# A hybrid encoder layer on one core: the first row blocks multiplied for two column chunks in turn, and the conversions of the start reordered

## The chip, the cores and the metric

One core of a Trainium2 chip runs the whole layer in one launch. Five engines work side by side: TensorE (PE) multiplies, VectorE (DVE) and ScalarE (ACT) do elementwise work, GpSimd (POOL) sets a few constants, SyncE (SP) issues nearly all transfers from the chip's memory. The metric is the device time of an execution in microseconds. A measurement of this kernel can tell apart differences of about 0.2%, some 2.3 us.

## The reference, cut to what matters

The layer takes 256 tokens of 2048 channels in 32-bit floats. Only its first product is touched by the change:

```
hn = rms_norm(h, g_mix_pre)          # h: 256 x 2048
u = hn @ w_in                        # w_in: 2048 x 5120
q, k, v, xr, yg = split(u)           # 1024 columns each
attn = neighborhood_attention(q, k, v, rpb)
rec = rglru_bidirectional(xr, ...) * gelu(yg)
mixed = concat(rms_norm(attn), rms_norm(rec)) @ w_out
...                                  # SwiGLU FFN, gated embedding, sandwich norms
```

## The kernel before, in words

**Products.** Each 32-bit factor is held as two parts, a high one rounded to the matmul's format (`wh` for weights, `hT_hi` for activations) and the rest (`wl`, `hT_lo`). A product is three matmuls: high by high, high by `wl`, `hT_lo` by `wh`. PE does them for 128 tokens and 512 columns at a time, accumulating over the 2048 channels in 16 blocks of 128.

**Weight tiles.** `w_in` is cut into ten *chunks* of 512 columns. A chunk is worked through in eight weight tiles, each with a pair of channel blocks (two blocks of 128 rows by 512 columns, 512 KB). A block takes six matmuls (three products for each of two groups of 128 tokens), a tile twelve. Chunk 0 (part of `xr`) goes first, then chunk 1 (part of `v`), and so on. The name `acc` is the accumulators of a chunk, two banks of PSUM.

**Streams of a weight tile.** `load_stream` issues its transfer on SP into one of four buffers `wr`; `hi_stream` casts it on ACT to `wh`; `lo_stream` subtracts on DVE and gives `wl`. There are six buffers for `wh` and `wl`. `pieces(i)` says whether tile `i` is handled whole or in two halves (a half is one channel block). Before, only tile 0 is halved.

**x.** The activations come transposed, as `xs`: pair `k` of channel blocks ahead of weight tile `k`. `make_hT` scales each block on ACT (L311, `hT_hi`) and takes the rest on DVE (L313, `hT_lo`). The tokens once more, untransposed (`xn`), come ahead of tiles 8 to 11; `norm_x` sums their squares and gives `rstd_x`, by which the chunks' results are scaled when they leave `acc`. `decay` works out small constants (`la`, `c8`) for the recurrence. `warm_up` runs seven matmuls on zeros before any data is there.

**After a chunk.** Chunk 0 is scaled on ACT into `ev`, transposed on DVE, sent through memory (`via`) and back, and copied into `xp`; eight DVE steps of a convolution make `xc`, whose two parts `xch` and `xcl` go into the gate matmuls `pg`. Chunk 1 is scaled into `vh` on ACT (L1136) and `vl` on DVE (L1140).

**What sets the order.** Matmuls of the tiles are written out in order. All other work is in small tasks, and while the program is built, a planner (`Plan`) plays through a model of time with costs per operation: each time it takes the task that can start earliest, shifted by the task's `late` (negative is more urgent), and writes its next instruction. Each engine then works strictly in that written order. A task added with a ready time is not considered earlier. `plan.clk["dma"]` is the time from which the model's transfers run, at 340 KB per us with 2 us to landing.

## Time and profile before

| what | us |
|---|---|
| median of 3 runs | 1155.36 |
| lowest, highest | 1154.85, 1156.58 |
| the profiled execution | 1154.11 |
| its span, first to last instruction | 1152.3 |
| PE busy | 1137.1 |
| DVE busy | 973.5 |
| ACT busy | 701.1 |

The span is what the trace shows; the execution's own time is 1.8 us more. Matmuls are pipelined: one of 512 columns is shown with a duration of 0.39 us, while the next starts 0.23 us after it, so the pace is read from the starts. "Idle before" is the time for which an engine stood still ahead of an instruction, with what released it. SPq is the queue on which SP issues transfers. Weight tiles are counted from 0, matmuls of the accumulators from 1.

### The profile page before, as it was taken

How to read it: one execution, taken by the hardware profiler on the slowest of the kernel's cores; microseconds unless marked ns; L12 is line 12 of the kernel's file. 1: busy time of each engine (PE TensorE's matmuls, PEld its weight loads, DVE VectorE, ACT ScalarE, POOL GpSimd, SP SyncE). 2: the span in 40 equal slices, each digit the busy share in tenths (PEclk: the TensorE clock that was granted, in tenths of full speed). 3: DMA queues.
4: the chain of work that ended last, by engine and by line, in shares of the span. 5: the costliest groups of instructions: out<-in, count | busy, mean ns of one | idle time of the engine just before them, and what ended most of it. 6: DMA issues, size and time to landing. Idle time of an engine off the chain costs nothing.

```text
span 1152.3 us, 14571 instructions
## 1 busy us (share of the span) xinstructions
PE 1137.1 (99%) x5138; PEld 942.0 (82%) x5138; DVE 973.5 (84%) x1266; ACT 701.1 (61%) x939; POOL 1.6 (0%) x13
## 2 busy tenths in 40 slices
PE   8999999999999999999999999999999999999996
PEld 6888888887888888888888888888888888888885
DVE  6668788789558898999977889999987999888996
ACT  7776888866548645474455555556444556466863
POOL 0000000000000000000000000000000000000000
PEclk9999999999999999999999999999999999999999
DMA  9876766576974877577775675668675757875661
GB/s 342 294 227 194 261 206 199 152 233 192 346 224 162 279 231 260 190 250 238 235 225 173 201 241 184 210 229 267 204 241 178 218 188 224 303 278 209 185 199 73
DMA packets 83305, 257.68 MB, mean 224 GB/s; under 512 B 8992, under 2 KB 24736, under 8 KB 81824
## 3 DMA queue, kind: packets, MB, share of 16 engines
q1 hardware_dynamic: 83088, 256.67, 68.8%
q8 instruction: 40, 0.66, 0.2%
q14 instruction: 33, 0.27, 0.1%
q10 hardware_dynamic: 144, 0.08, 0.0%
HBM read 242.04 MB, written 14.68 MB: 223 GB/s over the span
## 4 chain that ended last, share of the span: by engine, by line
PE 91%; DVE 3%; DMA 2%; ACT 2%; issue 1%; SPq 1%; DVEq 0%; ACTq 0%
PE c L558 15%; PE c L556 15%; PE c L557 15%; PE acc L557 9%; PE acc L558 9%; PE acc L556 9%; PE p L565 3%; PE p L567 3%; PE p L566 3%; PE c L565 2%; PE c L567 2%; PE c L566 2%; DVE wl L518 1%; DMA ev<-via 1%; ACT wh L508 1%
## 5 line engine op out<-in xcount | busy, mean ns | idle before, releaser
L518 DVE TENSOR_TENSOR wl<-wr,wh 128x1024 fp32r<-128x1024 f32 (+1 forms) x315 | 364.7, 1178 | 58.0 <-ACT wh L508 57.0
L508 ACT CAST wh<-wr 128x1024 fp32r<-128x1024 f32 (+1 forms) x315 | 314.1, 1018 | 141.7 <-PE c L558 50.5
L556 PE MATMUL c<-wh,hT_mix_hi 128*128 128x512 f32 x412 | 160.7, 390 | 0.0
L558 PE MATMUL c<-wh,hT_mix_lo 128*128 128x512 f32 x412 | 160.4, 389 | 0.0
L557 PE MATMUL c<-wl,hT_mix_hi 128*128 128x512 f32 x412 | 160.3, 389 | 0.0
L508 ACT CAST wh<-lent_t 128x1024 fp32r<-128x1024 f32 x69 | 72.3, 1053 | 130.3 <-DVE lent_t L542 96.4
L556 PE MATMUL acc<-wh,hT_hi 128*128 128x512 f32 x320 | 126.4, 395 | 1.8 <-ACT wh L508 1.8
L557 PE MATMUL acc<-wl,hT_hi 128*128 128x512 f32 x320 | 125.5, 392 | 1.5 <-DVE wl L518 1.5
L558 PE MATMUL acc<-wh,hT_lo 128*128 128x512 f32 x320 | 125.4, 392 | 0.0
L518 DVE TENSOR_TENSOR wl<-lent_t,wh 128x1024 fp32r<-128x1024 f32 x69 | 83.1, 1220 | 13.3 <-ACT wh L508 12.8
L558 PEld LDWEIGHTS c<-wh,hT_mix_lo 128*128 128x128 f32 x412 | 77.3, 188 | 16.3 <-DVE hT_mix_lo L313 0.2
L557 PEld LDWEIGHTS c<-wl,hT_mix_hi 128*128 128x128 f32 x412 | 77.4, 188 | 15.9
L556 PEld LDWEIGHTS c<-wh,hT_mix_hi 128*128 128x128 f32 x412 | 77.3, 188 | 15.8
L557 PEld LDWEIGHTS acc<-wl,hT_hi 128*128 128x128 f32 x320 | 60.4, 189 | 14.7 <-DVE wl L518 2.9
L556 PEld LDWEIGHTS acc<-wh,hT_hi 128*128 128x128 f32 x320 | 60.5, 189 | 14.4 <-ACT wh L508 2.4
L558 PEld LDWEIGHTS acc<-wh,hT_lo 128*128 128x128 f32 x320 | 60.4, 189 | 12.7
L508 ACT CAST wh<-lent_r 128x1024 fp32r<-128x1024 f32 (+1 forms) x57 | 55.7, 989 | 24.7 <-PE c L558 21.4
L518 DVE TENSOR_TENSOR wl<-lent_r,wh 128x1024 fp32r<-128x1024 f32 (+1 forms) x57 | 64.8, 1142 | 5.0 <-ACT wh L508 4.9
L556 PE MATMUL c<-wh,mid1h 128*128 128x512 f32 x84 | 32.7, 389 | 0.0
L557 PE MATMUL c<-wl,mid1h 128*128 128x512 f32 x84 | 32.7, 389 | 0.0
L558 PE MATMUL c<-wh,mid1l 128*128 128x512 f32 x84 | 32.7, 389 | 0.0
L565 PE MATMUL p<-wh,sums_f 128*128 128x512 f32 x80 | 31.1, 389 | 0.0
(501 smaller groups left out, 2331.4 us busy)
## 6 DMA issues: line engine op xcount, KB each, us to landing
wr<-in_w_in SPq DMA_DIRECT2D x79, 512.0 KB, 4.6
wr<-in_w_ffn_down SPq DMA_DIRECT2D x70, 512.0 KB, 4.8
wr<-in_w_ffn_gate SPq DMA_DIRECT2D x64, 512.0 KB, 4.5
wr<-in_w_ffn_up SPq DMA_DIRECT2D x64, 512.0 KB, 4.4
wr<-in_w_out SPq DMA_DIRECT2D x32, 512.0 KB, 5.0
lent_r<-in_w_ffn_up SPq DMA_DIRECT2D x24, 512.0 KB, 3.9
lent_r<-in_w_ffn_gate SPq DMA_DIRECT2D x24, 512.0 KB, 4.5
wr<-in_w_ple_gate SPq DMA_DIRECT2D x24, 512.0 KB, 4.5
```

Of the source, the lines that this page charges most:

```text
L508: nc.scalar.copy(his[i][:, j, :], raws[i][:, j, :])
L518: nc.vector.tensor_tensor(out=los[i][:, j, :], in0=raws[i][:, j, :], in1=f32(his[i][:, j, :]), op=ALU.subtract,)
L556: nc.tensor.matmul(accs[t], hi[t], wh[:, j, :], start=st, stop=False)
L557: nc.tensor.matmul(accs[t], hi[t], wl[:, j, :], start=False, stop=False)
L558: nc.tensor.matmul(accs[t], lo[t], wh[:, j, :], start=False, stop=sp)
L565: nc.tensor.matmul(o, lh, wh, start=start, stop=False)
L566: nc.tensor.matmul(o, lh, wl, start=False, stop=False)
L567: nc.tensor.matmul(o, ll, wh, start=False, stop=stop)
```

## The change

It does five things, all at the start of the program.

1. Tiles 0 and 1 are now the first pair of channel blocks for chunk 0 and for chunk 1; then come the other seven pairs for chunk 0, then those for chunk 1. Both chunks' accumulators are open from the start.
2. Tiles 0, 1 and 2 are loaded and converted in halves.
3. The x pairs 1 to 7 are loaded ahead of tiles 2 to 8 (before: 1 to 7), the `xn` ahead of tiles 9 to 12.
4. `make_hT` is less urgent (-1.0, before -1.4), `decay` is ready only at 20, and the planner's model has transfers start at 0.7 and books 440 KB more ahead of tile 0's second half (nothing is transferred for it).
5. One more matmul on zeros stands behind the first six matmuls.

```diff
+TURNS = 1
+HALVED = 3
+DECAY = 20.0
+HT_LATE = -1.0
+XN_FROM = 9
+FIRST_KB = 440
+FILL = {(0, 0): 1}
...
-        return [slice(0, 1), slice(1, 2)] if i == 0 else [slice(0, 2)]
+        return [slice(0, 1), slice(1, 2)] if i < HALVED else [slice(0, 2)]
...
             for j in pieces(i) if i not in singles else [slice(0, 2)]:
+                if not i and j.start:
+                    yield dma(FIRST_KB)
...
                 free_w(i)
+            for _ in range(FILL.get((i, j), 0)):
+                dummy()
             plan.run()
...
-        for j in pieces(k):
-            extra_loads.setdefault((k, j.start), []).append(load_xs(k, j))
+        i = 2 * k if k < TURNS else k + TURNS
+        for j in [slice(0, 1), slice(1, 2)] if not i else [slice(0, 2)]:
+            extra_loads.setdefault((i, j.start), []).append(load_xs(k, j))
     for i in range(2 * NT):
-        extra_loads.setdefault((8 + i, 0), []).append(load_xn(i))
+        extra_loads.setdefault((XN_FROM + i, 0), []).append(load_xn(i))
...
+        if n == 1:
+            for k in KS[:TURNS]:
+                for ch, c0 in firsts:
+                    seg(ch, "w_in", c0, hT, [k], first=k == KS[0], last=False)
+            for ch, c0 in firsts:
+                seg(ch, "w_in", c0, hT, KS[TURNS:], first=not TURNS)
+        elif n:
+            seg(chunk, "w_in", n0, hT, KS, after=start_biases if n == 3 else None)
...
+    plan.clk["dma"] = 0.7
...
-    plan.add(make_hT(0), late=-2 * LATE)
-    plan.add(make_hT(1), late=-2 * LATE)
+    plan.add(make_hT(0), late=HT_LATE)
+    plan.add(make_hT(1), late=HT_LATE)
     plan.add(norm_x(), late=NORM_X)
-    plan.add(decay())
+    plan.add(decay(), DECAY)
```

Below, names carry the program's buffer numbers, which differ between the two builds, and line numbers of the changed kernel are 7 to 15 higher. SP at the start, before (`xs0` is the half of the x blocks with pairs 0 to 3; a row of 128x512 is half a weight tile or a whole x pair):

```order
L665 DMA xs0_80<-in_xT 128x256
L483 DMA wr_115<-in_w_in 128x512
L665 DMA xs0_80<-in_xT 128x256
L483 DMA wr_115<-in_w_in 128x512
L665 DMA xs0_80<-in_xT 128x512
L483 DMA wr_125<-in_w_in 128x1024
L665 DMA xs0_80<-in_xT 128x512
L483 DMA wr_140<-in_w_in 128x1024
```

and after:

```order
L676 DMA xs0_80<-in_xT 128x256
L492 DMA wr_114<-in_w_in 128x512
L676 DMA xs0_80<-in_xT 128x256
L492 DMA wr_114<-in_w_in 128x512
L492 DMA wr_131<-in_w_in 128x512 x2
L676 DMA xs0_80<-in_xT 128x512
L492 DMA wr_138<-in_w_in 128x512 x2
L676 DMA xs0_80<-in_xT 128x512
L492 DMA wr_156<-in_w_in 128x1024
```

Two halves of the next weight tile moved ahead of the second x pair. ACT at the start, before (L721 is the first step of `decay`):

```order
L721 ACT_TABLE_LOAD
L721 ACTIVATE la0_105<-vec_69 128x16
L311 ACTIVATE hT0_hi_78<-xs0_80,vec_69 128x256
L508 CAST wh_122<-wr_115 128x512
L311 ACTIVATE hT0_hi_78<-xs0_80,vec_69 128x256 x2
L508 CAST wh_122<-wr_115 128x512
L311 ACTIVATE hT0_hi_78<-xs0_80,vec_69 128x256
L508 CAST wh_144<-wr_125 128x1024
```

and after:

```order
L318 ACT_TABLE_LOAD
L318 ACTIVATE hT0_hi_78<-xs0_80,vec_69 128x256
L517 CAST wh_119<-wr_114 128x512
L318 ACTIVATE hT0_hi_78<-xs0_80,vec_69 128x256
L517 CAST wh_119<-wr_114 128x512
L517 CAST wh_147<-wr_131 128x512 x2
L318 ACTIVATE hT0_hi_78<-xs0_80,vec_69 128x256
L517 CAST wh_167<-wr_138 128x512
L318 ACTIVATE hT0_hi_78<-xs0_80,vec_69 128x256
L517 CAST wh_167<-wr_138 128x512
L318 ACTIVATE hT0_hi_78<-xs0_80,vec_69 128x256 x2
L517 CAST wh_194<-wr_156 128x1024
```

The second half tile's cast now stands behind one x block of its own pair, where it stood behind the first block of the next pair; `la` has left. DVE follows in the same order with `hT_lo` and `wl`. ACT at the end of chunk 1, before (L723 is decay's second step, L843 the copies into `xp`):

```order
L723 ACT_TABLE_LOAD
L723 ACTIVATE la0_105<-la0_105 128x16
L508 CAST wh_494<-wr_465 128x1024
L508 CAST wh_509<-wr_477 128x1024
L508 CAST wh_549<-wr_518 128x1024
L843 COPY xp_335<-ev_424 128x8x4x8 x2
L508 CAST wh_565<-wr_532 128x1024
L843 COPY xp_335<-ev_424 128x8x4x8
L1136 ACTIVATE vh_351<-acc0_367,rstd_x_84 128x512
L843 COPY xp_335<-ev_424 128x8x4x8
L1136 ACTIVATE vh_351<-acc1_368,rstd_x_84 128x512
L508 CAST wh_595<-wr_543 128x1024
```

and after:

```order
L735 ACT_TABLE_LOAD
L735 ACTIVATE la0_105<-la0_105 128x16
L517 CAST wh_527<-wr_489 128x1024
L517 CAST wh_543<-wr_508 128x1024
L1151 ACTIVATE vh_373<-acc0_158,rstd_x_84 128x512
L1151 ACTIVATE vh_373<-acc1_159,rstd_x_84 128x512
L858 COPY xp_357<-ev_452 128x8x4x8 x4
L517 CAST wh_614<-wr_541 128x1024
L517 CAST wh_627<-wr_565 128x1024
L517 CAST wh_633<-wr_581 128x1024
```

Both `vh` moved ahead of all four copies and of the casts of tiles 20 to 22. On PE the sequence of kinds of matmuls is the same as before but for the one on zeros; only the tiles' order in the first two chunks differs.

More of the change, by code (lines that the diff above doesn't have):

```diff
@@ L755, in decay, with dummy @@
         done(ev_c8)
+    some, to = xn[0][:, 0:P], bank("warm")[:, 0, 0:P]
+    def dummy():
+        nc.tensor.matmul(to, some, some, start=True, stop=True)
     def warm_up():
-        some = xn[0][:, 0:P]
         nc.vector.memset(some, 0.0)
-        to = bank("warm")[:, 0, 0:P]
         for _ in range(WARM):
-            nc.tensor.matmul(to, some, some, start=True, stop=True)
+            dummy()
     t1 = {}
@@ L1206, in start_biases @@
         plan.add(load_biases(), plan.clk["pe"])
+    firsts = []
     for n, (n0, post) in enumerate((
@@ L1213, in layer @@
         late = SOON if n >= SOON_FROM else 0.0
-        seg(Chunk(post, (open_p1, second_tiles)[n] if n < 2 else None, late), "w_in", n0, hT, KS,
-            after=start_biases if n == 3 else None)
+        chunk = Chunk(post, (open_p1, second_tiles)[n] if n < 2 else None, late)
+        if n < 2:
+            firsts.append((chunk, n0))
+        if n == 1:
[6 more added lines that the diff above has]
+            seg(chunk, "w_in", n0, hT, KS, after=start_biases if n == 3 else None)
+    last_in = len(segs) - 1
     t2 = {}
@@ L1917, in layer @@
             run_seg(s)
-            if n == 9:
+            if n == last_in:
                 ev_in.t = plan.clk["pe"]
```

## The prediction

> **What bounds the kernel now.** I read the engine shares first, then the waits of PE, then the chain of work, and last the first 16 us instruction by instruction. Whole page, one later window, and the waits of PE (us in total, times, longest):

> ```profile
> PE 1137.1 (99%) x5138; PEld 942.0 (82%) x5138; DVE 973.5 (84%) x1266; ACT 701.1 (61%) x939; POOL 1.6 (0%) x13
> ...
> 400.00:600.00 200.00, 200.00 (x884) 165.62 (x883) 182.86 (x214) 107.78 (x119) 0.00 (x0) 1.00 0.71 230
> ...
> PE acc L556 <- ACT wh L508: 1.8, 2, 1.1
> PE acc L557 <- DVE wl L518: 1.5, 3, 1.0
> ...
> PE pb_rec L968 <- DVE ssr L983: 0.7, 1, 0.7
> ```

> The middle of the kernel is matmuls end to end: 884 in 200 us, 0.226 us each. All of PE's waits on weight halves (1.8 and 1.5 us) are on `acc`, and the timeline puts them ahead of 12.5 us. What is left is far later and small, such as the 0.7 at `pb_rec`. So the change, which touches only the start, can win what the start loses and no more. The chain of work shows how that loss is made (start, us, what):

> ```profile
> 2.59 4.50 DMA xs<-in_xT
> ...
> 7.11 0.51 ACT hT_hi L311
> 7.62 0.51 ACT wh L508
> 8.12 0.41 ACT hT_hi L311
> 8.54 0.93 ACT wh L508
> ...
> 9.91 0.89 DVE hT_lo L313 x2
> 10.80 1.15 DVE wl L518
> ...
> 11.99 0.79 PE acc L557
> ```

> Until 7.1 us the chain waits for the second x block; then it goes through the conversions on ACT and DVE to 12 us. The same stretch in the timeline (start, duration, engine, idle before and its releaser):

> ```profile
> 1.05 3.21 PE L762 MATMUL warm<-xn 128*128 128x128 f32 x14 [1.05 <-DVE xn L759]
> ...
> 3.28 0.22 ACT L721 ACTIVATE la<-vec 128x16 f32<-128x16 f32 x1 [0.83 <-DMA vec<-in_vecs]
> 3.40 0.49 ACT L311 ACTIVATE hT_hi<-xs,vec 128x256 fp32r<-128x256 f32 x1
> ...
> 4.20 0.62 ACT L508 CAST wh<-wr 128x512 fp32r<-128x512 f32 x1 [0.31 <-DMA wr<-in_w_in]
> ...
> 4.85 0.69 DVE L518 TENSOR_TENSOR wl<-wr,wh 128x512 fp32r<-128x512 f32 x1 [0.44 <-ACT wh L508]
> ...
> 4.87 0.50 PE L556 MATMUL acc<-wh,hT_hi 128*128 128x512 f32 x1 [0.62 <-ACT wh L508]
> ...
> 5.60 0.50 PE L557 MATMUL acc<-wl,hT_hi 128*128 128x512 f32 x1 [0.23 <-DVE wl L518]
> ...
> 5.76 0.51 ACT L311 ACTIVATE hT_hi<-xs,vec 128x256 fp32r<-128x256 f32 x1 [0.94 <-DMA xs<-in_xT]
> ...
> 6.30 0.48 DVE L313 SCALAR_TENSOR_TENSOR hT_lo<-xs,vec,hT_hi 128x256 fp32r<-128x256 f32 x1 [0.75 <-ACT hT_hi L311]
> ...
> 6.63 0.40 PE L558 MATMUL acc<-wh,hT_lo 128*128 128x512 f32 x1
> ...
> 7.11 0.51 ACT L311 ACTIVATE hT_hi<-xs,vec 128x256 fp32r<-128x256 f32 x1 [0.84 <-DMA xs<-in_xT]
> 7.52 0.60 ACT L508 CAST wh<-wr 128x512 fp32r<-128x512 f32 x1
> ...
> 8.97 0.68 DVE L518 TENSOR_TENSOR wl<-wr,wh 128x512 fp32r<-128x512 f32 x1
> ...
> 9.71 0.50 PE L557 MATMUL acc<-wl,hT_hi 128*128 128x512 f32 x1 [1.03 <-DVE wl L518]
> ...
> 14.27 0.40 PE L556 MATMUL acc<-wh,hT_hi 128*128 128x512 f32 x1
> ```

> The first half tile is multiplied from 4.87 to 6.86. The seventh matmul could go when the second half is converted; but its cast stands on ACT behind the second x block (7.11), and on DVE its low half comes 8.97 to 9.65, behind three x blocks. So the eighth matmul starts at 9.71 and not some 2 us before. And then PE runs at half clock. PE busy, PEld, DVE, ACT, POOL, granted clock, DMA share and GB/s:

> ```profile
> 3.97:7.39 3.42, 2.22 (x9) 1.14 (x7) 1.62 (x3) 1.41 (x3) 0.00 (x0) 1.00 0.91 319
> 7.39:10.80 3.41, 1.59 (x6) 1.11 (x7) 2.46 (x6) 3.29 (x7) 0.00 (x0) 1.00 1.03 404
> 10.80:14.21 3.41, 3.15 (x8) 2.03 (x7) 3.41 (x6) 2.73 (x5) 0.00 (x0) 0.50 1.03 363
> 14.21:17.60 3.39, 3.39 (x16) 2.75 (x15) 3.00 (x5) 2.81 (x5) 0.00 (x0) 1.00 0.98 369
> ```

> The stretch in which PE was busy 1.59 of 3.41 us is followed by one of the same length at clock 0.50. From 14.27, the 19th matmul, nothing waits until far later. In this execution the start thus costs 14.27 - 18 x 0.227 = 10.18 us ahead of a stream that never stops.

> **The change, part by part.**

> *Order of loads.* The first four transfers stay. Fifth and sixth are now the halves of chunk 1's first weight tile, where the second x block (256 KB) and a whole tile stood. The fifth was 256 KB before and is so now, so it lands at 7.08 as the x block did. From then on I take 404 GB/s (row 7.39:10.80): 256 KB in 0.65 us. Landings: tile 1 at 7.08 and 7.73, x pair 1 at 8.38, tile 2 at 9.03 and 9.68, x pair 2 at 10.33. By the 363 GB/s of the next row, tile 3 (512 KB, 1.44 us) lands at 11.77. The two more issues on SP cost nothing as long as an issue is shorter than a landing (0.65); by the nearest row, four `ev` issues in 2.18 us further below, one takes 0.55, and were the two not hidden, it is 1.1 us.

> [...]

> *ACT and DVE at the start.* The small `la` activation leaves the front: 3.40 becomes 3.28, hidden, since the cast at 4.20 waits for its landing. The second half's cast moves ahead of the second x pair. It landed by about 6.45 (5.76 plus 0.65), so cast 6.48 to 7.08, low half 7.11 to 7.80: 1.85 us earlier than 9.65. The other ends, by the rows' durations (half cast 0.60, x block 0.50, half low 0.68, x low 0.48): tile 1's low halves at 8.4 and 9.1, x block 2 low 9.5, tile 2's at 10.3 and 11.3, x block 3 low 10.7, tile 3 (whole: cast about 1.0 from 11.8, low 1.2) at 14.1. Two halves in place of a whole cost ACT 1.2 for 1.0 and DVE 1.37 for 1.2, twice: all of it beside PE's work, which has 24 matmuls (5.4 us) on the first x pair instead of 12.

> *PE.* Matmuls 1 to 6 as before. The seventh could go at 7.13, the eighth, on the low half, at 7.85. The extra warm-up matmul is two instructions, each at most the 3.21 / 14 = 0.23 us of the first ones: 0.46 us from 6.86 to 7.32. Then the seventh goes 0.2 later and still ends ahead of 7.85, so the cost is nothing; without that wait it would be up to 0.46. Then tile 0 ends at 8.98; tile 1 needs 8.4 and 9.1 at 8.98 and 10.34; tile 2 needs 10.3 and 11.3 at 11.70 and 13.06; tile 3 needs 14.1 at 14.42. No wait, the last by 0.3 us. The 19th matmul starts at 7.85 + 11 x 0.227 = 10.34.

> **Sum:** 14.27 - 10.34 = 3.93 us. About 1.7 of it is the stretch at half clock (3.41 / 2), which goes because PE is busy from 7.85 on; the rest are the two longest waits (1.1 and 1.0 in the list) and a small one, less the 0.5 that PE still waits ahead of the eighth. The most that could be won: no wait after 5.60 puts the eighth matmul at 6.96, a gain of 4.8.

> *Decay later, norm later, chunks 0 and 1 nearer together.* The decay chain, ready at 20, stays off the path. Chunk 1 now ends at 7.85 + 185 x 0.227 = 49.8 instead of 53.7, and what hangs on it is the next thing that could be late:

> ```profile
> 42.03 2.18 SPq L349 DMA_DIRECT2D ev<-via  x4
> ...
> ev<-via SPq DMA_DIRECT2D x4, 128.0 KB, 6.1
> ...
> 51.70 1.22 ACT L843 COPY xp<-ev 128x256 f32<-128x256 f32 x2
> ...
> 54.31 0.67 ACT L1136 ACTIVATE vh<-acc,rstd_x 128x512 fp32r<-128x512 f32 x1
> ...
> 55.63 0.42 DVE L880 TENSOR_SCALAR xc<-xp,vec 128x256 f32<-128x256 f32 x1 [2.57 <-ACT xp L843]
> ...
> 57.49 0.75 DVE L1140 SCALAR_TENSOR_TENSOR vl<-acc,rstd_x,vh 128x512 fp32r<-128x512 f32 x1
> ...
> 64.65 0.69 DVE L307 TENSOR_TENSOR xcl<-xc,xch 128x512 fp32r<-128x512 f32 x1
> ...
> 67.34 0.28 PE L362 MATMUL pg<-xch,gh 128*128 128x256 f32 x1
> ```

> The gate matmuls (`pg`) stand after 252 matmuls, as before: needed at 7.85 + 245 x 0.227 = 63.4, not 67.3. ACT now does both `vh` (from 49.9), then the four `xp` copies, then three casts: copies end at 49.9 + 6 x 0.6 = 53.5. From the first `xc` to the end of `xcl` it was 65.34 - 55.63 = 9.7 us; one weight half (1.15) and two `vl` (1.3) leave that stretch, four small decay steps of at most 0.48 enter: 7.3 to 9.2, I take 8 (these steps are 16 columns wide, far below the `xc` row). So `xcl` is there at 61.5, 1.9 us early; before it was 2.0. The weight half behind them, tile 20, comes at about 58.6 and is needed at 60.7. `ev` lands by 44.2 + 6.1 = 50.3; the norm behind it has one weight tile more ahead in the queue, up to 1.3 us later, which the copies (from 51.2) mostly cover. Hence zero; without cover each us late is a us of PE.

> After some 70 instructions on ACT and DVE the two programs run in the same order to the end, so nothing else is priced. The profiled execution took 1154.11 us for a span of 1152.3, the median of the runs is 1.25 above it. 1154.11 - 3.93 = 1150.2 for such an execution; for the median 1155.36 - 3.93 = **1151.4 us**.

> **Rivals.**

> *Half clock all the same.* If the stretches that decide the clock lie otherwise in the changed kernel, one at 0.50 costs up to 3.41 / 2 = 1.7 us; gain 2.2, 1153.2 us. For: PE still waits at 6.9 and 7.4. Against: the stretch 3.97:7.39, busy 2.22 of 3.42, kept the clock, and the changed start has no stretch emptier. [...]

> *Conversions late.* Tile 3 has 0.3 us to spare and tile 2 about 1.4; with landings a tenth slower, 0.5 to 1.5 us are lost: 1152.0 to 1153.0.

> *Given back at the second chunk.* The `pg` matmuls or tile 20 late by 2 to 4 us because `ev`, the norm or the gate weights land later: 1153.4 to 1155.4, no change by the measure of 0.2% (2.3 us), about what a measurement of this kernel can tell from no change.

> *Slower.* One place: ACT holds three casts (tiles 20 to 22) and the copies behind the two `vh`, which wait for chunk 1's last matmul. If `ev` lands so late that tile 20 comes after 60.7 + 3.9 + 2.3 = 66.9, it ends over 0.2% slower, near 1158. That asks for 8 us more than worked out; the `ev` rows show nothing like it.

> **Chances.** Clean start 0.62 (own range 1150.2 to 1152.4: 0.5 for the terms and the spread of the runs); half clock 0.12; conversions late 0.12; given back 0.09; slower 0.05. Half clock lies on the border, a third of it counted faster: faster 0.78, same 0.17, slower 0.05. Eight in ten: up to the half-clock case and a little beyond, down to the 4.8 bound: 1150.0 to 1153.8.

> **What would show it.** Right: the eighth matmul near 7.85, no clock below 1.00 between 8 and 15 us, no PE wait after 8 us until past 60, `pg` at 63.4. Wrong: a 0.50 stretch, PE waiting on tile 3's `wl` near 14, or a wait before `pg` or tile 20.

## The result, and the profile after

| | before | changed |
|---|---|---|
| median of 21 runs, us | 1155.32 | 1153.56 |
| lowest, highest | 1153.36, 1156.86 | 1151.73, 1155.4 |
| the profiled execution | 1154.11 | 1152.21 |
| its span | 1152.3 | 1150.4 |

The ratio is 0.9983 [0.9976, 0.9990]: 1.76 us faster, 0.17%. That is clear of no change at all, but under the 0.2% from which the forecast speaks of a faster kernel. The forecast was 3.93 us. So the kernel gains a little under half of what was worked out, and lies 2.2 us above the forecast value of 1151.4.

The engines' shares on the page of the changed kernel:

```profile
PE 1137.2 (99%) x5140; PEld 942.9 (82%) x5140; DVE 973.9 (85%) x1268; ACT 701.5 (61%) x941; POOL 1.6 (0%) x13
```

PE is busy as long as before (1137.1) with the two instructions on zeros more, so the 1.9 us of span are idle time that went. The waits of PE (engine and what it waits for: us in total, times, longest):

```profile
PE acc L565 <- ACT wh L517: 1.1, 1, 1.1
...
PE pb_rec L983 <- DVE ssr L998: 0.7, 1, 0.7
PE acc L565 <- ACT attn_hi L312: 0.5, 1, 0.5
```

The waits on weight halves that came to 1.8 and 1.5 us are one wait of 1.1. By this list alone the change has done nearly all it could. The timeline of the start tells what the list does not (start, duration, engine and line, idle before and its releaser):

```profile
1.05 3.35 PE L772 MATMUL warm<-xn 128*128 128x128 f32 x14 [1.05 <-DVE xn L775]
...
3.17 1.28 ACT L318 ACT_TABLE_LOAD   x1 [3.17 <-DMA xs<-in_xT]
...
4.47 0.51 ACT L318 ACTIVATE hT_hi<-xs,vec 128x256 fp32r<-128x256 f32 x1
4.88 0.60 ACT L517 CAST wh<-wr 128x512 fp32r<-128x512 f32 x1
...
5.54 0.79 PE L565 MATMUL acc<-wh,hT_hi 128*128 128x512 f32 x1 [1.13 <-ACT wh L517]
...
6.26 0.80 PE L566 MATMUL acc<-wl,hT_hi 128*128 128x512 f32 x1
...
7.28 0.63 PE L565 MATMUL acc<-wh,hT_hi 128*128 128x512 f32 x1
...
7.71 0.63 PE L566 MATMUL acc<-wl,hT_hi 128*128 128x512 f32 x1
...
8.56 0.63 PE L772 MATMUL warm<-xn 128*128 128x128 f32 x2
...
8.84 0.77 PE L565 MATMUL acc<-wh,hT_hi 128*128 128x512 f32 x1
...
9.41 0.58 PE L566 MATMUL acc<-wl,hT_hi 128*128 128x512 f32 x1
...
10.06 0.40 PE L565 MATMUL acc<-wh,hT_hi 128*128 128x512 f32 x1
...
12.13 0.39 PE L565 MATMUL acc<-wh,hT_hi 128*128 128x512 f32 x1
```

Two things are to be seen. The first product starts at 5.54, where it started at 4.87 before: ACT loads its table from 3.17 to 4.45, and until that is done the first x block and the first cast cannot go. Then PE waits for nothing, and yet the matmuls start 0.43 us apart (7.28, 7.71), at half pace; from 10.06 on they start 0.23 apart. A wait is not the only way to lose time: at half pace PE loses 0.20 us with each matmul here (0.43 for 0.23), and that stands in no list of waits. The eighth matmul starts at 9.41, forecast 7.85; the 19th at 12.13, forecast 10.34, before 14.27.

The stretches of the clock, counted from its border at 9.80 in steps of 3.41 us, the length of the half stretch of before; that the step holds where no border is recorded is the author's reading (PE, PEld, DVE, ACT and POOL busy with the instructions begun, granted clock, DMA share, GB/s):

```profile
2.97:6.38 3.41, 2.28 (x9) 1.54 (x8) 1.23 (x3) 2.81 (x4) 0.00 (x0) 1.00 0.82 262
6.38:9.80 3.42, 3.42 (x9) 2.79 (x10) 2.78 (x5) 2.63 (x5) 0.00 (x0) 1.00 0.97 362
9.80:13.21 3.41, 3.41 (x16) 2.79 (x15) 2.64 (x7) 3.21 (x7) 0.00 (x0) 1.00 1.02 410
```

Here the clock column is not to be trusted: the trace's first record of the clock is at 9.80, and ahead of it the view prints 1.00. The counts tell: 9 matmuls in a busy stretch ahead of 9.80, 16 in the next. In the profile of before the clock was full from 3.98 to 10.80 and 0.50 from there to 14.21, with matmuls 0.43 apart (13.01, 13.44); in the changed kernel they are 0.43 apart up to 9.80, so it is read as half up to there. The stretch at half clock was not removed, it moved.

Behind the start nothing is given back at the second chunk. The gate matmuls (min, median and max duration in ns, start of the first and the last in us):

```profile
L369 PE MATMUL pg<-xch,gh x8: 277/283/283, 65.2 to 73.1; 128*128 128x256 f32 x8
```

They begin at 65.17, where before it was 67.34: 2.17 us earlier, against 2.14 at the 19th matmul. The spans differ by 1.9.

### The profile page after: what moved, and what is told of

Read it like the earlier page. It is cut to its first block, busy times and chain, and to the rows that moved or that the text cites. A ratio compares the mean times of both kernels' runs of the same rounds, so it can differ in the third digit from the quotient of the medians.

```text
span 1150.4 us, 14584 instructions
## 1 busy us (share of the span) xinstructions
PE 1137.2 (99%) x5140; PEld 942.9 (82%) x5140; DVE 973.9 (85%) x1268; ACT 701.5 (61%) x941; POOL 1.6 (0%) x13
## 4 chain that ended last, share of the span: by engine, by line
PE 94%; DVE 2%; DMA 2%; ACT 1%; issue 0%; SPq 0%; DVEq 0%; ACTq 0%
PE c L567 15%; PE c L565 15%; PE c L566 15%; PE acc L565 10%; PE acc L566 10%; PE acc L567 10%; PE p L577 3%; PE p L578 3%; PE p L576 3%; PE c L577 2%; PE c L578 2%; PE c L576 2%; DVE wl L527 1%; DMA ev<-via 1%; PE tr L332 0%
## 5 line engine op out<-in xcount | busy, mean ns | idle before, releaser
L566 PEld LDWEIGHTS acc<-wl,hT_hi 128*128 128x128 f32 x320 | 60.5, 189 | 12.6 <-DVE wl L527 0.6
```

Source lines behind the costliest of these rows:

```text
L566: nc.tensor.matmul(accs[t], hi[t], wl[:, j, :], start=False, stop=False)
```

## The experiments

Five theories went in. A: ACT's table load, which stood ahead of `decay`'s first step and started at 1.17, now stands ahead of the first x activation and takes over its wait for the x block (3.17). B: the gap on PE behind the warm-up grew from 0.62 to 1.13 us, the stretch 2.97:6.38, busy 2.28 us, did not release the clock (the matmuls behind it stayed 0.43 apart), and the loss is the clock's. C: the loss is in the order of the casts and landings, and not in the clock. D: the start gains, and later waits take it back. E: what differs between profiled executions later on is chance. The table has every run that follows; the medians of the experiments are of 5 to 12 runs, each ratio is to the kernel before on the same chip, and the places are of the profiled execution, in us.

| run | median | ratio | first / eighth / 19th matmul | full clock from | `pg` |
|---|---|---|---|---|---|
| before (profiled) | 1155.32 | | 4.87 / 9.71 / 14.27 | 3.98, half 10.80 to 14.21 | 67.34 |
| changed | 1153.56 | 0.9983 [0.9976, 0.9990] | 5.54 / 9.41 / 12.13 | 9.80 | 65.17 |
| e0 changed, again | 1152.72 | 0.9976 [0.9967, 0.9984] | 5.58 / 9.45 / 12.37 | 10.32 | 65.41 |
| e1 table first | 1152.85 | 0.9980 [0.9969, 0.9992] | 4.69 / 8.57 / 11.54 | 9.53 | 64.58 |
| e2 table first, 8 warm-ups | 1152.64 | 0.9977 [0.9968, 0.9985] | 4.63 / 8.02 / 10.66 | 4.36 | 63.70 |
| e4 same as e2 | 1153.01 | 0.9979 [0.9970, 0.9988] | 4.68 / 8.65 / 11.30 | 4.72 | 64.34 |
| e5 10 warm-ups | 1152.05 | 0.9972 [0.9961, 0.9983] | 5.43 / 7.89 / 10.51 | 5.34 | 63.55 |
| e9 same as e5 | 1152.30 | 0.9977 [0.9968, 0.9986] | 5.55 / 8.23 / 10.89 | 4.22 | 63.93 |
| e10 table first, 10 warm-ups | 1153.62 | 0.9988 [0.9979, 0.9996] | 5.09 / 8.46 / 11.11 | 4.82 | 64.15 |
| e11 4 warm-ups | 1153.91 | 0.9989 [0.9980, 0.9998] | 5.48 / 9.36 / 13.00 | 11.74 | 66.06 |
| e3 before, `decay` late | 1154.84 | 0.9996 [0.9988, 1.0005] | 5.69 / 9.99 / 13.54 | 4.96 | 66.58 |
| e8 before, 10 warm-ups | 1155.55 | 1.0003 [0.9994, 1.0012] | 5.34 / 9.70 / 13.23 | 5.88 | 66.30 |
| e6 as e2, one tile halved | 1161.34 | 1.0049 [1.0036, 1.0062] | 4.65 / 8.09 / 11.62 | 4.87 | other order |
| e7 as e6, no turns | 1159.05 | 1.0033 [1.0020, 1.0045] | 4.65 / 8.22 / 12.42 | 4.82 | other order |

**e0, the changed kernel once more.** No edit.

> The changed kernel once more, unchanged, beside the next three. Theory A: of the 1.8 us that the forecast of 3.9 lost, a fixed part comes from the table load on ACT, which now stands behind the wait for the first x block (3.17 to 4.45 us), so that the first matmul of the accumulators starts near 5.54 instead of 4.87; this comes out the same here. Theory B: the rest is the stretch of PE at half clock, whose border lay at 9.80 in the first profile and lies elsewhere from execution to execution; then the border moves here, by anything up to 3.4 us, and the 19th matmul with it (12.13 at the first profile, between 11.0 and 12.6 here). Rival C: the loss is in the order of the casts and landings and not in the clock; then the border and the 19th matmul come out as in the first profile. Time 1153.6, ratio to before 0.998.

It shows the same start: first product at 5.58, half pace until 10.32, 19th matmul at 12.37. So the late release of the clock is no accident of the first profile. It hardly tells B from C: the border moved, as B asks, but only by 0.52, and the 19th matmul by 0.24.

**e1, the table loaded first.** A copy of one column needs no data from memory, and the load goes with it.

```diff
+    lead = const.tile([P, 1], F32, name="lead")
+    nc.scalar.copy(lead, eps)
     warm_up()
```

> The changed kernel with one 1-column copy of a constant ahead of all on ACT, so that the table load waits for no transfer. Theory A: table load ends before 3.1, first matmul at 4.85 to 4.95, PE's idle time behind the warm-up 0.5 instead of 1.1 us. With the clock's border at 9.80 as in the first profile the 19th matmul then starts 0.36 us earlier (0.67 us earlier, at half clock), at 11.8; if the clock is full from 7.4 on or sooner it is 10.3 to 10.7. Time 1151.5 to 1153.3. Rival C, landings decide: first matmul stays later than 5.2, time as the changed kernel's within 0.4.

Timeline of e1:

```profile
1.17 1.28 ACT L1926 ACT_TABLE_LOAD   x1 [1.17 <-PEq L2013]
...
4.02 0.62 ACT L517 CAST wh<-wr 128x512 fp32r<-128x512 f32 x1
4.69 0.79 PE L565 MATMUL acc<-wh,hT_hi 128*128 128x512 f32 x1 [0.28 <-ACT wh L517]
...
8.57 0.63 PE L566 MATMUL acc<-wl,hT_hi 128*128 128x512 f32 x1
...
11.54 0.39 PE L565 MATMUL acc<-wh,hT_hi 128*128 128x512 f32 x1
```

The load is back at 1.17 and the first product at 4.69, 0.85 earlier: theory A is right on where the load went and what it held up. But the first matmul still takes 0.79, the clock is half until 9.53, and at the 19th matmul 0.59 is left. A alone does not explain the start. Nor is the width of the gap on PE the reason, as B had it: it is 0.28 here, less than the 0.62 of before, and the clock is released late all the same, at 9.53.

**e2 and e4, table first and one warm-up matmul more.**

```diff
-WARM = 7
+WARM = 8
```

> As the one before, with eight matmuls on zeros at the start instead of seven, which fill PE's idle time from 4.4 to 4.9. Theory B: PE is then busy without a gap from 1.05 to some 5.1, a whole stretch of 3.41 us is full at the latest by 7.9 and the clock is full from there; the runs scatter less than the changed kernel's (1151.7 to 1155.4), and the time is 1151 to 1152.5. Rival C: no gain over seven matmuls, or 0.2 us of loss where the eighth delays the first product.

> The kernel with the early table load and eight warm-up matmuls once more: its first profile had the 19th matmul at 10.66 and the gate matmuls at 63.70 (forecast 10.34 and 63.4), yet its time was only that of the changed kernel, with PE waits of 0.7 near 382 us on lent_w and 0.6 near 535 on wl that the first profile of the changed kernel does not have. Theory D: what is won at the start is partly taken back there, whenever PE comes early; then both waits recur here and the time is 1152.3 to 1153. Rival E: those waits are chance, of 0 to 1 us in any execution; then they differ here, the median lies at 1151.5 to 1152.3, and the execution's time follows from the start plus that chance.

Timeline of e2:

```profile
4.63 0.49 PE L565 MATMUL acc<-wh,hT_hi 128*128 128x512 f32 x1
...
8.02 0.49 PE L566 MATMUL acc<-wl,hT_hi 128*128 128x512 f32 x1 [0.23 <-DVE wl L527]
...
10.66 0.39 PE L565 MATMUL acc<-wh,hT_hi 128*128 128x512 f32 x1
```

Now the first product takes 0.49 where it took 0.79, the clock being full from 4.36, and the 19th starts at 10.66, 0.88 earlier than in e1. That the one warm-up matmul more brought this about is not shown: the borders happened to fall at 4.36 and 4.72, and in e3, below, the clock was full from 4.96 behind seven. The start is nearly the forecast one (10.34); in e4, where PE waited 0.9 us for the second half tile's cast (0.3 in e2) and the seventh matmul went at 7.92 in place of 7.29, it is 11.30. The time does not follow: e2's median, 1152.64, was forecast at 1151 to 1152.5, and its ratio, 0.9977, is that of e0 on the same chip, 0.9976, though its start is 1.7 earlier. That is what D and E are about, below.

**e5 and e9, only the longer warm-up.** The table load stays where the change put it.

```diff
-WARM = 7
+WARM = 10
```

> The changed kernel with ten matmuls on zeros at the start instead of seven and nothing else, so that PE is busy without a gap from 1.05 to about 5.6 while the table load stays late. Theory B, the clock is released by a full stretch of 3.41 us: PE is at full clock from 7.9 at the latest (9.80 and 10.32 in the changed kernel's profiles), the first matmul of acc starts at 5.55 to 5.7, the 19th at 10.9 to 11.6 instead of 12.1 to 12.4, the gate matmuls at 64.0 to 64.8 instead of 65.2 to 65.4. Rival: the clock does not follow from PE's activity at the start; border again beyond 9.

> The changed kernel with ten warm-up matmuls once more, to hold the best time so far against another profile and more runs. Theory B: clock full from before 7.9, eighth matmul 7.8 to 8.2 (later only if the second half tile lands late), 19th at 10.4 to 11.0, gate matmuls 63.4 to 64.1, time 1151.4 to 1152.7, ratio 0.997. If the first result was chance: 19th above 11.5 or time above 1153.

Timeline of e5:

```profile
1.05 4.54 PE L772 MATMUL warm<-xn 128*128 128x128 f32 x20 [1.05 <-DVE xn L775]
...
3.07 1.28 ACT L318 ACT_TABLE_LOAD   x1 [3.07 <-DMA xs<-in_xT]
...
5.43 0.49 PE L565 MATMUL acc<-wh,hT_hi 128*128 128x512 f32 x1
...
7.89 0.49 PE L566 MATMUL acc<-wl,hT_hi 128*128 128x512 f32 x1
...
10.51 0.39 PE L565 MATMUL acc<-wh,hT_hi 128*128 128x512 f32 x1
```

The stretch of its clock ahead of the border (columns as above):

```profile
1.93:5.34 3.41, 3.41 (x18) 3.41 (x17) 0.43 (x1) 2.26 (x3) 0.22 (x1) 1.00 0.87 241
```

Its gate matmuls:

```profile
L369 PE MATMUL pg<-xch,gh x8: 277/282/283, 63.6 to 71.5; 128*128 128x256 f32 x8
```

With the load as late as in the changed kernel (3.07) and the first product as late (5.43), the eighth matmul starts at 7.89 (forecast 7.85), the 19th at 10.51 (10.34) and `pg` at 63.55 (63.4). The stretch 1.93:5.34 is full of warm-up matmuls, and the clock is full behind it. With seven they would have ended at 4.40, as in the changed kernel. So the loss is the clock's, 12.13 less 10.51, 1.62 us (e0 less e9: 1.48), and C falls, since ACT, DVE and PE do the same work in the same order in both. The medians are the lowest of the study too: 1152.06 over both runs (18 runs), against 1153.18 of the changed kernel (31 runs) and 1155.21 of before (105 runs). But these are runs on several chips, and the ratios to before on the same chip, 0.9972 and 0.9977, lie too near to the 0.9983 and 0.9976 of the changed kernel: that ten are faster than seven is shown for the start, not for the time of the whole.

**e10, both.** Table first and ten warm-ups.

> Ten warm-up matmuls and the early table load together. If the late table load costs only by the gap that it leaves in PE's work (and so by the clock), it costs nothing once PE has no gap: first matmul near 5.4 in both, eighth at 7.8 to 8.2, 19th at 10.4 to 11.0, time as with ten warm-up matmuls alone within 0.5. If it costs by itself, the 19th comes 0.3 us or more earlier than 10.51 and the time is 0.5 to 0.7 lower.

The 19th matmul starts at 11.11, not ahead of e5's 10.51 or e9's 10.89: under full clock the early load is worth nothing here, since PE stands for the second half tile in any case (0.82 us ahead of the seventh matmul, 0.22 ahead of the eighth). The median of 1153.62 is 1.3 above e9's on the same chip, where at most 0.5 had been forecast, though the starts differ by 0.2. Its waits of PE on this:

```profile
PE pb_rec L983 <- DVE ssr L998: 1.1, 1, 1.1
PE c L566 <- DVE lent_w L527: 1.1, 1, 1.1
```

Both are far behind the start, at some 270 and 380 us, and 1.5 larger together than the 0.7 at `pb_rec` of the profile after, which has no `lent_w`. Whether the early load brings this about or the runs fell so is open.

**e11, a shorter warm-up.**

```diff
-WARM = 7
+WARM = 4
```

> The changed kernel with four matmuls on zeros instead of seven, so that PE stands still from about 2.9 to 5.5. Theory B: no stretch of 3.41 us is full before 5.5, full clock comes at 9 to 12.4 us, the 19th matmul at 12.0 to 13.6, time 1153 to 1154.8, that is 0 to 1.5 us above the changed kernel and 1 to 2.5 above ten warm-up matmuls. Rival, the warm-up does not matter: as the changed kernel, clock border anywhere.

Timeline of e11:

```profile
5.48 0.80 PE L565 MATMUL acc<-wh,hT_hi 128*128 128x512 f32 x1 [2.35 <-ACT wh L517]
```

The stretch ahead of its border (columns as above):

```profile
8.33:11.74 3.41, 3.41 (x10) 2.74 (x10) 3.18 (x7) 3.22 (x7) 0.00 (x0) 1.00 1.02 399
```

PE stands 2.35 us ahead of the first product, the clock is released only at 11.74, and the 19th matmul starts at 13.00. Ten, seven and four warm-ups give borders at 5.34, 9.80 and 11.74 and a 19th matmul at 10.51, 12.13 and 13.00, with the first product within 0.11 of the same place. These three alone are no proof, since the border differs between executions of one kernel (5.34 and 4.22 with ten). But the stretches of e11 and of e3, below, lie almost alike: with four warm-ups the one that ends at 4.91, counted back from 11.74, holds 1.63 us of work and does not release the clock (the first product takes 0.80), with seven the one that ends at 4.96 holds 2.86 and does (0.49). The time agrees: 1153.91 with four and 1152.30 with ten (e9), 11 runs each on the same chip.

**e3, the kernel before with the table load late.** `decay` is held back as the change does; all else is old.

```diff
-    plan.add(decay())
+    plan.add(decay(), 20.0)
```

> The kernel before with the decay chain alone ready at 20, as the change has it; it moves the table load behind the first x block. Theory A: first matmul at 5.5 instead of 4.87; but the second half tile's cast stands behind the second x pair there (7.52 in the trace of before), so matmuls 8 and on come as before, within 0.3 us, if the clock's stretches lie alike. Time as before within 0.7 us. Rival: the late table load costs the old order its full 0.7 us or more, also at the 19th matmul.

Timeline of e3:

```profile
3.32 1.28 ACT L311 ACT_TABLE_LOAD   x1 [3.32 <-DMA xs<-in_xT]
...
9.99 0.50 PE L557 MATMUL acc<-wl,hT_hi 128*128 128x512 f32 x1 [1.03 <-DVE wl L518]
```

The load moves to 3.32 here too, the first product to 5.69, and nothing is lost: the eighth matmul waits 1.03 for DVE in any case, and the ratio is 0.9996 [0.9988, 1.0005]. So the late load costs the old order nothing. In the new one it costs 0.59 under half clock (e1) and nothing under full clock (e10).

This execution had a full clock from 4.96, with no half stretch behind it. The stretch ahead of that border (columns as above):

```profile
1.55:4.96 3.41, 2.86 (x14) 2.56 (x12) 0.00 (x0) 1.62 (x2) 0.60 (x3) 1.00 0.67 202
```

This corrects B. The gap on PE is 1.28 us here, wider than the 1.13 of the changed kernel, behind the same seven warm-ups. They end at 4.40, so only 0.56 of the gap lies ahead of the border. In the changed kernel the borders fell so that the stretches 2.97:6.38 and, in e0, 3.49:6.90 have the whole gap inside. In before the stretch 0.56:3.97 ended ahead of its gap. By these executions it is the place of the border, which differs between executions of one kernel (9.80 and 10.32, 5.34 and 4.22), that decides whether seven warm-ups release the clock, and not the growth of the gap from 0.62 to 1.13.

**e8, the kernel before with ten warm-ups.**

```diff
-WARM = 7
+WARM = 10
```

> The kernel before with ten matmuls on zeros at the start instead of seven, nothing else. If the clock at the very start were all that matters, this gains as the changed kernel did with them (1.4 us or more). By the theory it gains nothing: the old order keeps PE waiting until 9.7 for the eighth matmul whatever the clock, and the quiet stretch between 7 and 10 us can bring the half clock back after it. Eighth matmul at 9.5 to 9.9, 19th at 12.3 to 14.5, time within 0.7 us of before.

Timeline of e8:

```profile
8.16 0.50 PE L556 MATMUL acc<-wh,hT_hi 128*128 128x512 f32 x1 [0.94 <-ACT wh L508]
...
9.70 0.50 PE L557 MATMUL acc<-wl,hT_hi 128*128 128x512 f32 x1 [1.03 <-DVE wl L518]
```

With no half clock from 5.88 on, the old order still reaches its 19th matmul only at 13.23, and the time does not change. In the old order the longer warm-up is worth nothing that shows.

**e6 and e7, parts taken away.** Both are e2 with less of the change: e6 halves only tile 0, e7 also has no turns between the chunks.

```diff
-HALVED = 3
+HALVED = 1
```

> The kernel with early table load and eight warm-up matmuls, but tiles 1 and 2 whole again (only tile 0 halved); the planner then writes another order up to some 270 us, so only the start is compared. By the rows: tile 1 (512 KB) lands at 7.7, cast to 8.8, low half to 10.0, while tile 0 ends at 9.0: PE waits 1.0 us there, the 19th matmul comes at 11.4 instead of 10.66, the gate matmuls' place 0.7 later. Rival: the halves are worth nothing, since PE is busy with tile 0 until then (at half clock it would be): 19th at 10.7.

```diff
-TURNS = 1
-HALVED = 3
+TURNS = 0
+HALVED = 1
...
-XN_FROM = 9
+XN_FROM = 8
```

> As the one before, and the tiles in the old order too (chunk 0 alone first, x pair 1 ahead of tile 1): of the change only the casts ahead of x, the planner's landings and the late decay are left. Another order up to some 270 us, so only the start is compared. By the rows: eighth matmul at 7.9 to 8.1 as with the turns, tile 0 ends at 9.1; tile 1 lands at 8.34, cast to 9.4, low half to 10.6; 19th matmul at 12.0, 1.3 us behind the kernel with turns and halves and 2.2 us ahead of the kernel before. Rival: the casts' order is the whole of the gain, 19th at 10.7.

Timeline of e6, then of e7:

```profile
10.37 0.50 PE L566 MATMUL acc<-wl,hT_hi 128*128 128x512 f32 x1 [0.63 <-DVE wl L527]
...
11.62 0.39 PE L565 MATMUL acc<-wh,hT_hi 128*128 128x512 f32 x1
```

```profile
9.89 0.49 PE L565 MATMUL acc<-wh,hT_hi 128*128 128x512 f32 x1 [0.22 <-ACT wh L517]
...
11.15 0.50 PE L566 MATMUL acc<-wl,hT_hi 128*128 128x512 f32 x1 [0.76 <-DVE wl L527]
```

In e6 PE stands ahead of tile 1, which is converted whole, and the 19th matmul, forecast at 11.4, is 1.0 later than in e2: that is what the halves of tiles 1 and 2 are worth (the seventh matmul goes at nearly the same time in both, 7.36 and 7.29, so the landings do not make the difference). In e7 PE stands for the second pair's tile as well, and the 19th is at 12.42 (forecast 12.0), 0.8 later again: what the turns are worth. Against executions of the old order without a half stretch (13.54 and 13.23) the cast that goes ahead of the x blocks is worth the last 0.8 to 1.1. All three parts of the change do their work at the start. The sizes are rough, each being from one execution: the 19th matmul of one and the same kernel moved by 0.24 (changed, e0), 0.38 (e5, e9) and 0.64 (e2, e4). The times of e6 and e7 (1161.34, 1159.05) do not price these parts: the planner wrote another order for both, different up to some 270 us. In e7 PE waits 3.49 us ahead of the matmul at 281.77, and those from 282.36 to 284.49 start 0.43 apart, at half pace once more.

**D and E: where the rest of the gain goes.** From the first gate matmul to the first matmul of the embedding (`acc<-bw`, near 1128) the profiled executions took 1061.81 (before), 1062.07 (changed), 1062.36, 1063.21, 1064.92, 1062.77, 1062.72 and 1062.49 (e0 to e5), 1063.54, 1062.56, 1064.78 and 1062.95 (e8 to e11). The builds with the old order (before, e3, e8) have a mean of 1062.7, those with the new one 1063.1. e5 and e9 bring PE there early (63.55 and 63.93) and take 1062.5, so an early start is not paid back as a rule, as D had it. Yet the four builds with the early table load (e1, e2, e4, e10) have a mean of 1063.9 and the five others of the new order 1062.5. That goes with their times, which are no better than the changed kernel's for all that their starts are earlier. Whether the early load brings it about is not shown: e2 and e4 are the same kernel and differ by 2.2 us. The waits of PE in e2, then in e4:

```profile
PE c L566 <- DVE lent_w L527: 0.7, 1, 0.7
PE pb_rec L983 <- DVE ssr L998: 0.7, 1, 0.7
PE p L577 <- DVE wl L527: 0.6, 1, 0.6
```

```profile
PE pb_rec L983 <- DVE ssr L998: 0.8, 1, 0.8
...
PE c L566 <- DVE lent_w L527: 0.3, 1, 0.3
```

The waits shown make up 0.9 of the 2.2. Set against e4 matmul by matmul, e2 loses 2.1 between 482 and 536 us, in five stops of 0.2 to 0.8, of which the list has only the one on `wl`; why they come there stays open. So there are a few places late in the kernel where PE has no slack, and there it waits 0 to 1.1 us as the execution falls. That is E, with one miss: the median of e4, 1153.01, lies at the upper end of what D had forecast (1152.3 to 1153) and above E's range. The profiled execution of before had the smallest time of all on this stretch, and lies 1.2 under its own median.

## Why the prediction was right or wrong

**Right, as e5 shows it.** With the clock released, the start comes out by the sum: 7.89, 10.51 and 63.55 where 7.85, 10.34 and 63.4 stood. In e9, the same kernel, the three places lie 0.4 to 0.6 behind the forecast. So the landings of the halves, the margins of tiles 1 to 3 and of `xcl` ahead of `pg`, and the zeros for `decay`, the norm and the issues on SP hold within 0.2 us in the one and 0.6 in the other. In the changed kernel the halves of tile 1 land near 7.0 and 7.7 and those of tile 2 near 9.5 and 10.1, against 7.08, 7.73, 9.03 and 9.68: with two more transfers they are at most 0.5 us behind. "Given back at the second chunk" and "Slower" did not happen.

**Wrong, step one:** "The small `la` activation leaves the front: 3.40 becomes 3.28, hidden". The row of 0.22 was priced, and the row ahead of it in the written order, the table load, was taken to stay. In these builds it stands ahead of whichever instruction is ACT's first (`la` in before, the x activation in the changed kernel, the copy in e1), and in the changed kernel it carried the wait for the x block: 3.17 to 4.45, first product 5.54 and not 4.87. The order lists quoted with the change show it as the first row of ACT, on another line than before. The load takes 1.28 us in both builds, and in the changed kernel the activation starts at 4.47, 0.02 behind its end.

**Wrong, step two:** of the 3.93, "about 1.7 of it is the stretch at half clock (3.41 / 2), which goes because PE is busy from 7.85 on", and in the rival "the changed start has no stretch emptier". Both looked at the stretches behind the warm-up alone. That full pace comes only at a first border, and that with seven warm-ups this border was early in some executions only (3.98 in before and 4.96 in e3, but 9.80 and 10.32 in the changed kernel), was not asked. The term did not go: it is the 1.62 us between the changed kernel and e5. Its size was off too: the way from the eighth to the 19th matmul took 4.56 us in before, with the half stretch, and 3.55 and 3.53 in e3 and e8, without one. So the half stretch of before cost 1.0 and not 1.7. The time came out as the rival "Half clock all the same" had it (1153.2, against 1153.56; 1153.18 over all runs), though not by its words: the half clock came ahead of the stream and not in a hole of it. That the number fits so well is partly luck, and that 1153.56 lies within 1150.0 to 1153.8 is owed to the range, which was drawn out to this rival; the clean start, which carried the forecast, did not come. A chance of 0.12 was too little for a clock that every execution shows at another place.

**Wrong, small:** the extra matmul on zeros, "so the cost is nothing". At half clock PE did not wait behind it, and it put the seventh matmul off from 8.56 to 8.84, 0.28 us. In e5 it is hidden, as worked out, or nearly so (the seventh goes at 7.58, the eighth waits for `wl` until 7.89). The second half's cast was put at 6.48 and starts at 6.42 in the changed kernel, 6.69 in e6 and 6.83 in e7; the seventh matmul could go at 7.3 to 7.9 and not at 7.13, worth 0.0 to 0.8 at the eighth.

**The base.** 3.93 was subtracted from the time of one execution and from the median alike. What the start gains does reach the end in the profiled pair (2.14 at the 19th matmul, 1.9 of span). But the execution of before had a half stretch, which e3 and e8 did not have, with a 19th matmul at 13.54 and 13.23. Against these even e5, which starts as forecast, gains 2.7 to 3.0 and not 3.93; its median and e9's are 3.4 and 2.5 below before on the same chip. And executions scatter by 1 us from the late waits, so a gain of 2 us shows only between medians of many runs.

## What to carry to other kernels

When an instruction leaves the front of an engine's queue, look at what stood with it: here the table load of 1.28 us went to the next activation and started at 3.17, with the x block, where it had started at 1.17. Ask at what pace PE goes ahead of the first product and behind it, and read it from the spacing of matmuls (0.43 or 0.23 us here), since the half clock stood in no list of waits. With ten warm-ups the clock was full from 4.22 to 5.88 in all four executions (e5, e8, e9, e10), with seven from 3.98 to 10.32 in five (before, changed, e0, e1, e3); so when a change puts the first product off, try a longer warm-up with it. Here that is ten matmuls for seven, and the lowest median of the study: 1152.06 for 1155.21 us, ratios 0.9972 [0.9961, 0.9983] and 0.9977 [0.9968, 0.9986], though not clear of the changed kernel's own. And do not take the base of a forecast from one execution: see first what in it was chance.

## What the runs showed of the hardware

The clock's border falls elsewhere in each execution: the first is at 9.80 and 10.32 in two of the changed kernel, 4.36 and 4.72 in e2 and e4, 5.34 and 4.22 in e5 and e9, though the first matmul on zeros starts at 1.05 in those shown. In before the borders lie at 3.98, 10.80, 14.21 and 1147.44, in the changed kernel at 9.80 and 1143.03: 6.82, 3.41 and 1133.2 us apart in the one, 1133.2 in the other, that is 2, 1 and 332 steps of 3.413. Ahead of the first border the matmuls on zeros go more slowly: the ten of e8 and of e9 (twenty instructions) take 4.63 us with the border at 5.88 and 4.00 with it at 4.22.

How busy PE was in the stretch ahead of the first full one is less uniform. That stretch in before and in e2 (columns as above):

```profile
0.56:3.97 3.41, 2.92 (x13) 2.92 (x14) 0.21 (x2) 1.90 (x3) 1.39 (x9) 1.00 0.58 158
```

```profile
0.95:4.36 3.41, 3.31 (x15) 3.31 (x16) 0.48 (x2) 2.38 (x4) 1.17 (x8) 1.00 0.63 176
```

And the stretch before the last ahead of the border, behind which the clock was not yet full, in e0 and in e1:

```profile
3.49:6.90 3.41, 2.24 (x8) 1.41 (x7) 1.18 (x2) 2.52 (x4) 0.00 (x0) 1.00 0.83 251
```

```profile
2.70:6.12 3.42, 3.14 (x12) 2.31 (x11) 1.18 (x2) 1.41 (x3) 0.00 (x0) 1.00 0.86 249
```
